# Four instead of three seven-product pairs per slab in the gate and up projections, and another order of the pairs

## The chip, the core and the metric

The kernel runs on one core of one Trainium2 chip. The engines that matter are TensorE (PE, matrix products), VectorE (DVE) and ScalarE (ACT) for element-wise work, GpSimd (POOL) for more of it, and SyncE (SP), which issues the weight transfers. The metric is the device time of one execution in microseconds (us), lower is better: 2799.63 us before, the median of 3 runs (2798.4 to 2800.11).

## The reference, cut to what matters

One layer of a decoder on 256 tokens of width 2048, in float32: a SwiGLU feed-forward part (FF = 5632), a mixer of attention and a state-space scan, and a second SwiGLU part. The change touches the two feed-forward parts alone:

```python
def swiglu(x, w_gate, w_up, w_down):
    return (jax.nn.silu(x @ w_gate) * (x @ w_up)) @ w_down
...
f = swiglu(rms_norm(h, ffn1_pre_g[i]), ffn1_w_gate[i], ffn1_w_up[i], ffn1_w_down[i])
h = h + 0.5 * rms_norm(f, ffn1_post_g[i])
```

## The kernel before, in words

**Float32 in three products.** Each weight tile is split into a high part (ACT, L133, a copy to fp32r) and a low part (DVE, L134, the tile minus its high part); the activations are split in the same way once and kept in "slots". A float32 product is then three matrix products of 128 columns by 512: high by high, high by low, low by high (L389 to L391 in `gate_up`, L140 to L142 in `project`).

**Slabs and units.** FF is cut into 11 slabs of 512 columns. A slab of gate and up sums over 8 units; a unit p is one pair of 128-row blocks of the weights of gate and up, one transfer of 1 MB (128 x 4 x 512). There are two kinds:
- an ordinary unit (N below): 2 blocks x 2 token halves x (gate, up) = 8 float32 products, 24 instructions on PE; two splits of 128x1024 (parts a and b).
- a seven-product unit (S below, those p in the tuple `SP`): the four blocks form a 2x2 matrix product, which is done with 7 products of sums (Strassen's scheme in Winograd's form): 21 instructions on PE. POOL makes the sums of weights, four additions of 128x512 per unit (L371 in `Ahead.make`); three splits of 128x1024 (parts a, c, b) and one of 128x512 (part d), of which b and d read the sums `wsum` and c the block that POOL's fourth addition wrote. The sums of activations are made once, while slab 0 runs (`pair_slots.sums`, L343 to L347), for slab 0 has ordinary units only.

**Banks.** A slab with S units fills all 8 PSUM banks: four for the results g0, u0, g1, u1, and four (p1, p5, p6, p7) for products of the S units. After the last S unit, ACT copies p1 (L428) and DVE makes four combinations from p5, p6, p7 (L430 to L433, "the combinations"); that frees the four. At the slab's end DVE adds these to the results (L440, L442, "the closing adds"), ACT applies Silu (L445), DVE multiplies (L446).

**What sets the order.** `ORDER` is the order of the units in slabs 1 to 10, `SP` which are S. In `ffn` the slabs go in groups (0 to 2, 3 to 5, 6 to 8, 9 and 10); after each group come four slabs of the down projection (`project`). `flush`, called after a unit whose number stands in `after=`, transposes the previous slab's result (L217, tile tp, two banks) into a slot (ACT L197, DVE L198). `Ahead` loads and sums the weights of S units two units ahead, across slabs: two buffers raw7 (tag h) and two buffers wsum (tag xc). A raw7 is free for the next load when its part c is split. Splits of 128x1024 rotate through 4 buffers. Every engine takes its instructions in the order in which they are queued.

```python
            kind = p in SP[:-1]
            if kind not in self.free:
                self.free[kind] = new_slot()
...
            if p in sp:
                raw, e = coming.take()
...
            if len(self.made) == 2 or not self.units:
                return
```

Of the kernel before, what the change touches and what calls it, by code (L numbers as in the profile page):

```python
# [33 lines left out]
EPS = 1e-6  # L34
NFF = FF // S
NP = D // (2 * P)
SP = (2, 4, 6)
ORDER = (0, 2, 1, 4, 3, 6, 5, 7)
AHEAD = 300
LAMBDA_INIT = 0.8 - 0.6 * math.exp(-0.3 * 0)  # L40

# [10 lines left out]
def decoder_layer(ctx: ExitStack, tc: tile.TileContext, x, x_t, cols, rows, post_g, wgu1, wd1, w_in,  # L52
# [91 lines left out]
    def project(xs, w, n, by_token=0):  # L144

        ps = [psm.tile([P, S], F32, name="acc", tag="m") for _ in range(NT)]
        tail = []
        for c in range(len(xs)):  # L150
            raw = raws.tile([P, 4, S], F32, name="raw", tag=turn("raw", 3))
            loaded[0] = nc.sync.dma_start(raw, w(n, c))
            sl = xs[c] = xs[c]() if callable(xs[c]) else xs[c]
            for b in range(2):
                hi, lo = split(raw[:, 2 * b:2 * b + 2], [P, 2, S])
                for jj in range(2):
                    j = 2 * b + jj
                    tail.append((sl, j, hi[:, jj], lo[:, jj], c + j == 0, c == len(xs) - 1 and j == 3))
            if c < len(xs) - by_token:
                for sl_, j, wh, wl, first, last in tail:  # L160
                    for t in range(NT):
                        matmul3(ps[t], sl_, j, t, wh, wl, first, last)
                tail = []
        for t in range(NT):
            for sl_, j, wh, wl, first, last in tail:
                matmul3(ps[t], sl_, j, t, wh, wl, first, last)
        return ps
# [23 lines left out]
    def new_slot():  # L191
        return slots.tile([P, 4, 2, TT], F32R, name="slot")

    def fill(sl, j, src):

        js = slice(j, j + src.shape[1])
        nc.scalar.activation(sl[:, js, 0], src, AF.Copy)  # L197
        nc.vector.tensor_tensor(out=sl[:, js, 1], in0=src, in1=sl[:, js, 0].bitcast(F32), op=ALU.subtract)  # L198
# [10 lines left out]
    def to_slot(src, gain=None):  # L209

        sl = new_slot()
        for b in range(2):
            ps = psm.tile([P, 2, TT], F32, name="tp", tag="m")
            for k in range(2):
                for t in range(NT):
                    j = 2 * b + k
                    nc.tensor.transpose(ps[:, k, t * P:(t + 1) * P], src[t][:, j * P:(j + 1) * P], ident)  # L217
            if gain is None:
                fill(sl, 2 * b, ps)
            else:  # L220
                fill_gain(sl, 2 * b, ps, gain)
        return sl
# [81 lines left out]
    class pair_slots:  # L304
# [8 lines left out]
        def make(self, p, src, gain):  # L313

            g = col[:, gain + 2 * p:gain + 2 * p + 2]
            kind = p in SP[:-1]
            if kind not in self.free:
                self.free[kind] = new_slot()
                sl, k = self.free[kind], 0
            else:  # L320
                sl, k = self.free.pop(kind), 2
            self.at0[p] = sl, k
            if p in SP:
                xg = self.xg[p] = tmp.tile([P, 2, TT], F32, name="xg", tag="t2")
                for i in range(2):
                    nc.scalar.activation(xg[:, i], src[:, i], AF.Copy, scale=g[:, i:i + 1])
                fill(sl, k, xg)
            else:
                self.at[p] = sl, k
                for i in range(2):  # L330
                    nc.scalar.activation(sl[:, k + i, 0], src[:, i], AF.Copy, scale=g[:, i:i + 1])
                    nc.vector.scalar_tensor_tensor(
                        out=sl[:, k + i, 1], in0=src[:, i], scalar=g[:, i:i + 1],
                        in1=sl[:, k + i, 0].bitcast(F32), op0=ALU.mult, op1=ALU.subtract)
# [116 lines left out]
    def ffn(xo, scale, wgu, wd, gi, h_of, fetch=None):  # L451


        nonlocal h
        rs = []
        post = None
        todo = []
        groups = ((0, 3), (3, 6), (6, 9), (9, NFF))
        order = lambda j: ORDER
        coming = Ahead(wgu, [(j, p) for j in range(1, NFF) for p in order(j) if p in SP])  # L460

        def flush():
            if todo:
                hs.append(to_slot(todo.pop()))

        for a, b in groups:
            hs = []
            for j in range(a, b):
                if j == 0:
                    steps = dict(scale)  # L470

                    def behind(i):
                        if i in steps:
                            rs.append(steps[i]())
                        if i - 1 in SP:
                            xo.sums(i - 1)
                        if i >= NP - 2:
                            coming.behind = loaded[0]
                            coming.make()
                            coming.behind = None  # L480
                    todo.append(gate_up(xo.at0, wgu, 0, range(NP), (), None, lambda: rs[-1], fetch,
                                        {i: lambda i=i: behind(i) for i in range(NP)}))
                else:
                    todo.append(gate_up(xo.at, wgu, j, order(j), SP, coming, lambda: rs[-1], after={6: flush}))
            last = b == NFF
            if last:
                h = [hpool.tile([P, D], F32, name=f"h{t}", tag=f"h{t}") for t in range(NT)]
                for t in range(NT):
                    nc.gpsimd.dma_start(h[t], h_of(t))
            if not post:  # L490
                post = PostNorm(gi, 0.5)
                f = post.f

            def final():
                flush()
                return hs[-1]

            lazy = hs + [final]
            for n in range(4):
                pd = project(lazy, lambda n, c: wd[n, a + c], n, by_token=2 if last and n == 3 else 0)  # L500
                part = f[:, :, n * S:(n + 1) * S]
                if not last:
                    for t in range(NT):
                        if a == 0:
                            nc.scalar.activation(part[:, t], pd[t], AF.Copy)
                        else:
                            nc.vector.tensor_tensor(out=part[:, t], in0=pd[t], in1=part[:, t], op=ALU.add)
                else:
                    def get(t):
                        v = tmp.tile([P, S], F32, name="fsum", tag="t2")  # L510
                        nc.vector.tensor_tensor(out=v, in0=pd[t], in1=part[:, t], op=ALU.add)  # L511
                        return v
                    post.slab(n, get)
        return post.finish()
# [30 lines left out]

    steps1 = {i: lambda c=c: square1(c) for c, i in enumerate((1, 2, 4, 5))}
    update = ffn(x1, {**steps1, 7: scale1}, wgu1, wd1, 0, lambda t: x[t * P:(t + 1) * P], fetch1)


# [383 lines left out]
    for t in range(NT):  # L933
        nc.gpsimd.dma_start(hsave2[t], h[t])
    update = ffn(x2, {1: pre_scale}, wgu2, wd2, 2, lambda t: hsave2[t])
    for t in range(NT):
        for c in range(4):
# [57 lines left out]
```

## Time and profile before

| what | value |
|---|---|
| median of 3 runs | 2799.63 us |
| the profiled execution's own time | 2802.36 us |
| its span, first to last instruction | 2800.7 us |
| PE busy | 2769.4 us (99%) |
| DVE busy | 2058.7 us (74%) |
| ACT busy | 1450.1 us (52%) |
| POOL busy | 627.6 us (22%) |
| granted PE clock, mean | 0.996 |

How to read it: busy time is the union of an engine's instructions. Matrix products are pipelined, so one lasts longer (0.39 us) than the distance to the next. The shares are means over stages with different limits; the slabs of gate and up are one stage, the down projection and the mixer are others.

### The profile page before, as it was taken

The numbers are of one execution on the slowest core, as the hardware profiler recorded it, in microseconds if no ns is written. First come the engines' busy times: TensorE is split into PE (matmuls) and PEld (weight loads), VectorE is DVE, ScalarE is ACT, GpSimd is POOL, SyncE is SP. The second block draws the span as 40 slices with busy tenths as digits, with TensorE's granted clock in tenths as the row PEclk, the third lists the DMA queues.
The fourth block names the chain that finished last, engine by engine and source line by source line (L and its number), as shares of the span: only waits on it lengthen the run. The fifth ranks groups of instructions, "written<-read, shape, count | busy, mean of one in ns | idle before, by whom it ended". The sixth has DMA issues, their size and how long they took to land. (4 is left out here: it accounts for less than half of the span.)

```text
span 2800.7 us, 33759 instructions
## 1 busy us (share of the span) xinstructions
PE 2769.4 (99%) x13120; PEld 2312.7 (83%) x13120; DVE 2058.7 (74%) x2311; ACT 1450.1 (52%) x1822; POOL 627.6 (22%) x377
## 2 busy tenths in 40 slices
PE   8999999999999999999999999999999999999998
PEld 6888888888788888888788888888878888888887
DVE  7959969878688877777765565544568869789696
ACT  6545545545565556555444444444465555455454
POOL 2605415322012111111100000000015325236040
PEclk9999999999999999999999999999999999999999
DMA  6555555556555555555554445555556555555554
GB/s 259 206 189 204 198 182 208 195 185 214 198 190 179 189 182 192 184 186 194 188 183 167 176 170 180 203 190 191 193 199 226 194 187 205 196 195 196 195 205 156
DMA packets 77985, 541.50 MB, mean 193 GB/s; under 512 B 8768, under 2 KB 8912, under 8 KB 14080
## 3 DMA queue, kind: packets, MB, share of 16 engines
q1 hardware_dynamic: 73152, 519.08, 52.0%
q0 software_dynamic: 4528, 20.09, 2.0%
q8 instruction: 103, 1.69, 0.2%
q14 instruction: 58, 0.48, 0.0%
q10 hardware_dynamic: 144, 0.17, 0.0%
HBM read 532.94 MB, written 6.36 MB: 193 GB/s over the span
## 5 line engine op out<-in xcount | busy, mean ns | idle before, releaser
L134 DVE TENSOR_TENSOR w_lo<-raw,w_hi 128x1024 fp32r<-128x1024 f32 x978 | 1359.2, 1404 | 628.4 <-ACT w_hi L133 619.2
L133 ACT ACTIVATE w_hi<-raw 128x1024 fp32r<-128x1024 f32 x978 | 1035.7, 1060 | 1050.1 <-PE acc L142 581.6
L140 PE MATMUL acc<-w_hi,slot 128*128 128x512 f32 x1856 | 729.8, 393 | 0.8 <-DVE slot L205 0.2
L141 PE MATMUL acc<-w_lo,slot 128*128 128x512 f32 x1856 | 722.9, 389 | 0.0
L142 PE MATMUL acc<-w_hi,slot 128*128 128x512 f32 x1856 | 720.1, 390 | 0.0
L140 PEld LDWEIGHTS acc<-w_hi,slot 128*128 128x128 f32 x1856 | 348.9, 188 | 78.6 <-ACT slot L197 4.6
L142 PEld LDWEIGHTS acc<-w_hi,slot 128*128 128x128 f32 x1856 | 348.7, 188 | 73.1
L141 PEld LDWEIGHTS acc<-w_lo,slot 128*128 128x128 f32 x1856 | 348.9, 188 | 72.4 <-DVE y L731 1.2
L181 PE MATMUL acc<-slot,w_hi 128*128 128x512 f32 x1280 | 407.8, 399 | 0.2 <-ACT zs L775 0.2
L371 POOL TENSOR_TENSOR wsum<-raw 128x512 f32<-128x512 f32 x120 | 226.7, 1889 | 773.8 <-DMA raw<-in_wgu 766.7
L389 PE MATMUL gu<-w_hi,slot 128*128 128x512 f32 x928 | 363.4, 392 | 7.6 <-ACT w_hi L133 7.6
L390 PE MATMUL gu<-w_lo,slot 128*128 128x512 f32 x928 | 363.2, 391 | 2.6 <-DVE w_lo L134 2.5
L391 PE MATMUL gu<-w_hi,slot 128*128 128x512 f32 x928 | 362.8, 391 | 0.0
L183 PEld LDWEIGHTS acc<-slot,w_lo 128*128 128x128 f32 x1280 | 240.4, 188 | 56.1
L183 PE MATMUL acc<-slot,w_lo 128*128 128x256 f32 x1280 | 252.9, 278 | 0.0
L389 PEld LDWEIGHTS gu<-w_hi,slot 128*128 128x128 f32 x928 | 175.2, 189 | 43.5 <-ACT w_hi L133 7.6
L390 PEld LDWEIGHTS gu<-w_lo,slot 128*128 128x128 f32 x928 | 175.1, 189 | 40.2 <-DVE w_lo L134 4.1
L391 PEld LDWEIGHTS gu<-w_hi,slot 128*128 128x128 f32 x928 | 175.1, 189 | 36.6
L181 PEld LDWEIGHTS acc<-slot,w_hi 128*128 128x128 f32 x1280 | 196.6, 189 | 4.3 <-issue 2.4
L134 DVE TENSOR_TENSOR w_lo<-wsum,w_hi 128x1024 fp32r<-128x1024 f32 x120 | 167.5, 1435 | 19.5 <-ACT w_hi L133 18.9
L389 PE MATMUL gu<-w_hi,sums 128*128 128x512 f32 x420 | 163.4, 389 | 0.0
L390 PE MATMUL gu<-w_lo,sums 128*128 128x512 f32 x420 | 163.4, 389 | 0.0
(228 smaller groups left out, 2153.0 us busy)
## 6 DMA issues: line engine op xcount, KB each, us to landing
raw<-in_wgu SPq DMA_DIRECT2D x175, 1024.0 KB, 4.7
raw<-in_wd SPq DMA_DIRECT2D x88, 1024.0 KB, 4.8
raw<-in_w_in SPq DMA_DIRECT2D x80, 1024.0 KB, 4.8
raw<-in_w_in_t SPq DMA_DIRECT2D x80, 1024.0 KB, 4.8
raw<-in_w_ssm SPq DMA_DIRECT2D x32, 1024.0 KB, 4.7
raw<-in_w_att SPq DMA_DIRECT2D x16, 1024.0 KB, 4.7
raw<-in_w_out SPq DMA_DIRECT2D x16, 1024.0 KB, 4.7
dec<-acsD POOLq DMA_DIRECT2D x16, 512.0 KB, 5.1
```

The source lines that it names most:

```text
L133: split_last["hi"] = nc.scalar.activation(hi[:, js], raw[:, js], AF.Copy)
L134: split_last["lo"] = nc.vector.tensor_tensor(out=lo[:, js], in0=raw[:, js], in1=hi[:, js].bitcast(F32), op=ALU.subtract)
L140: nc.tensor.matmul(ps, xh, wh, start=first, stop=False)
L141: nc.tensor.matmul(ps, xh, wl, start=False, stop=False)
L142: nc.tensor.matmul(ps, xl, wh, start=False, stop=last)
L181: nc.tensor.matmul(ps[f], hi[:, j, wf[f]], sl[:, j], start=b + j == 0, stop=False)
L183: nc.tensor.matmul(ps[f][:, TT:], lo[:, j, wf[f]], sl[:, j, :TT], start=False, stop=b == len(xs) - 1 and j == 3)
L371: sum_last[0] = nc.gpsimd.tensor_tensor(out=o, in0=a, in1=b, op=ALU.add)
L389: nc.tensor.matmul(bank[k], xh, wh, start=done[k] == 1, stop=False)
L390: nc.tensor.matmul(bank[k], xh, wl, start=False, stop=False)
L391: nc.tensor.matmul(bank[k], xl, wh, start=False, stop=done[k] == count[k])
```

## The change: four S units, at places 1, 3, 4 and 6

`SP` becomes (1, 3, 4, 6) and `ORDER` the natural one, so a slab runs N0 S1 N2 S3 S4 N5 S6 N7, where it ran N0 S2 N1 S4 N3 S6 N5 N7. The last S unit is the seventh of eight now and was the sixth. `flush` is called after the last unit and not after the seventh. In `pair_slots.make` all S units share slots, before all but the last.

```diff
-SP = (2, 4, 6)
-ORDER = (0, 2, 1, 4, 3, 6, 5, 7)
+SP = (1, 3, 4, 6)
+ORDER = (0, 1, 2, 3, 4, 5, 6, 7)
...
-            kind = p in SP[:-1]
+            kind = p in SP
...
-                    todo.append(gate_up(xo.at, wgu, j, order(j), SP, coming, lambda: rs[-1], after={6: flush}))
+                    todo.append(gate_up(xo.at, wgu, j, order(j), SP, coming, lambda: rs[-1], after={7: flush}))
```

**First place: DVE in the middle of slab 1.** Names that end in raw7 or wsum on the right are parts of S units (a, c, b, d), those with raw parts of N units. Before:

```order
L134 TENSOR_TENSOR w_lo_628<-raw7_494,w_hi_627 128x1024
L134 TENSOR_TENSOR w_lo_632<-raw7_494,w_hi_631 128x1024
L134 TENSOR_TENSOR w_lo_636<-wsum_495,w_hi_635 128x1024
L134 TENSOR_TENSOR w_lo_640<-wsum_495,w_hi_639 128x512
L134 TENSOR_TENSOR w_lo_674<-raw_671,w_hi_673 128x1024
L134 TENSOR_TENSOR w_lo_678<-raw_671,w_hi_677 128x1024
L134 TENSOR_TENSOR w_lo_706<-raw7_561,w_hi_705 128x1024
L134 TENSOR_TENSOR w_lo_710<-raw7_561,w_hi_709 128x1024
L134 TENSOR_TENSOR w_lo_714<-wsum_562,w_hi_713 128x1024
L134 TENSOR_TENSOR w_lo_718<-wsum_562,w_hi_717 128x512
```

In the changed kernel, in the same stretch:

```order
L134 TENSOR_TENSOR w_lo_641<-raw7_507,w_hi_640 128x1024
L134 TENSOR_TENSOR w_lo_645<-raw7_507,w_hi_644 128x1024
L134 TENSOR_TENSOR w_lo_649<-wsum_508,w_hi_648 128x1024
L134 TENSOR_TENSOR w_lo_653<-wsum_508,w_hi_652 128x512
L134 TENSOR_TENSOR w_lo_685<-raw7_574,w_hi_684 128x1024
L134 TENSOR_TENSOR w_lo_689<-raw7_574,w_hi_688 128x1024
L134 TENSOR_TENSOR w_lo_693<-wsum_575,w_hi_692 128x1024
L134 TENSOR_TENSOR w_lo_697<-wsum_575,w_hi_696 128x512
L134 TENSOR_TENSOR w_lo_731<-raw_728,w_hi_730 128x1024
L134 TENSOR_TENSOR w_lo_735<-raw_728,w_hi_734 128x1024
```

Between two S units stood two splits of an N unit; now two S units follow each other, eight splits in a row, and the N unit comes behind them.

**Second place: DVE from the end of slab 1 into slab 2.** The combinations (L430 to L433), the slot of the previous result (L198) and the closing adds (L440, L442). Before (the splits with raw_808 are of the slab's last unit N7, those with raw_850 of the next slab's first unit):

```order
L134 TENSOR_TENSOR w_lo_811<-raw_808,w_hi_810 128x1024
L430 TENSOR_TENSOR u2_754<-gu_585,c_g0_749 128x512
L134 TENSOR_TENSOR w_lo_815<-raw_808,w_hi_814 128x1024
L431 TENSOR_TENSOR c_g1_750<-gu_589,u2_754 128x512
L432 TENSOR_TENSOR c_u0_751<-gu_581,u2_754 128x512
L433 TENSOR_TENSOR c_u1_752<-gu_581,c_g1_750 128x512
L134 TENSOR_TENSOR w_lo_853<-raw_850,w_hi_852 128x1024
L134 TENSOR_TENSOR w_lo_857<-raw_850,w_hi_856 128x1024
L198 TENSOR_TENSOR slot_793<-tp_794,slot_793 128x2x256
L198 TENSOR_TENSOR slot_793<-tp_801,slot_793 128x2x256
L440 TENSOR_TENSOR c_g0_749<-gu_517,c_g0_749 128x512
L134 TENSOR_TENSOR w_lo_889<-raw7_643,w_hi_888 128x1024
```

And in the changed kernel (raw_873 is the next slab's first unit, raw7_700 its first S unit):

```order
L134 TENSOR_TENSOR w_lo_876<-raw_873,w_hi_875 128x1024
L430 TENSOR_TENSOR u2_811<-gu_598,c_g0_806 128x512
L134 TENSOR_TENSOR w_lo_880<-raw_873,w_hi_879 128x1024
L431 TENSOR_TENSOR c_g1_807<-gu_602,u2_811 128x512
L432 TENSOR_TENSOR c_u0_808<-gu_594,u2_811 128x512
L433 TENSOR_TENSOR c_u1_809<-gu_594,c_g1_807 128x512
L134 TENSOR_TENSOR w_lo_912<-raw7_700,w_hi_911 128x1024
L440 TENSOR_TENSOR c_g0_806<-gu_530,c_g0_806 128x512
L442 TENSOR_TENSOR c_u0_808<-gu_534,c_u0_808 128x512
L440 TENSOR_TENSOR c_g1_807<-gu_538,c_g1_807 128x512
L134 TENSOR_TENSOR w_lo_916<-raw7_700,w_hi_915 128x1024
L198 TENSOR_TENSOR slot_850<-tp_851,slot_850 128x2x256
```

The combinations stood between the splits of the slab's last unit and stand now between those of the next slab's first; three of the closing adds come before the slot is filled, which they followed.

**Third place: PE at the transposes.** The last transpose and the products that follow; a new bank waits for DVE where "waits DVE" stands at a product's first row. Before (the slab's last unit N7 follows):

```order
L217 MATMUL tp_801<-ident_84,sg_504 128x128
L389 MATMUL gu_517<-w_hi_810,slot_390 128x512 [waits Activation_49]
L390 MATMUL gu_517<-w_lo_811,slot_390 128x512
L391 MATMUL gu_517<-w_hi_810,slot_390 128x512
L389 MATMUL gu_521<-w_hi_810,slot_390 128x512
L390 MATMUL gu_521<-w_lo_811,slot_390 128x512
L391 MATMUL gu_521<-w_hi_810,slot_390 128x512
L389 MATMUL gu_525<-w_hi_810,slot_390 128x512
L390 MATMUL gu_525<-w_lo_811,slot_390 128x512
L391 MATMUL gu_525<-w_hi_810,slot_390 128x512
L389 MATMUL gu_529<-w_hi_810,slot_390 128x512
```

In the changed kernel (the next slab's first unit follows):

```order
L217 MATMUL tp_858<-ident_84,sg_517 128x128
L389 MATMUL gu_883<-w_hi_875,slot_111 128x512 [waits DVE_49,Activation_49]
L390 MATMUL gu_883<-w_lo_876,slot_111 128x512
L391 MATMUL gu_883<-w_hi_875,slot_111 128x512
L389 MATMUL gu_887<-w_hi_875,slot_111 128x512 [waits DVE_49]
L390 MATMUL gu_887<-w_lo_876,slot_111 128x512
L391 MATMUL gu_887<-w_hi_875,slot_111 128x512
L389 MATMUL gu_891<-w_hi_875,slot_111 128x512 [waits DVE_49]
L390 MATMUL gu_891<-w_lo_876,slot_111 128x512
L391 MATMUL gu_891<-w_hi_875,slot_111 128x512
L389 MATMUL gu_895<-w_hi_875,slot_111 128x512 [waits DVE_49]
```

The transposes stood ahead of the last unit, which goes on with open banks; they stand now at the slab's end, where four new banks must be free, and all four wait for DVE.

## Rows read from the trace of the kernel before

**Rows 1.** Page, parts 1, 5 and 6: engines; POOL's first sums, 2 per unit; loads

```profile
PE 2769.4 (99%) x13120; PEld 2312.7 (83%) x13120; DVE 2058.7 (74%) x2311; ACT 1450.1 (52%) x1822; POOL 627.6 (22%) x377
...
L371 POOL TENSOR_TENSOR wsum<-raw 128x512 f32<-128x512 f32 x120 | 226.7, 1889 | 773.8 <-DMA raw<-in_wgu 766.7
...
raw<-in_wgu SPq DMA_DIRECT2D x175, 1024.0 KB, 4.7
```

**Rows 2.** Windows of a slab's length, slabs 3 and 4; columns in the first line

```profile
core 0: us, PE busy (x) PEld busy (x) DVE busy (x) ACT busy (x) POOL busy (x), PEclk, DMA share, GB/s
211.00:253.40 42.40, 42.40 (x189) 35.11 (x188) 37.52 (x29) 24.22 (x26) 24.37 (x12) 1.00 0.54 191
257.80:300.20 42.40, 42.40 (x193) 35.20 (x192) 41.95 (x35) 24.50 (x28) 23.87 (x12) 1.00 0.55 199
```

**Rows 3.** Timeline of PE, slab 5: first products of units, transposes, down projection

```profile
314.90 0.39 PE L389 MATMUL gu<-w_hi,slot 128*128 128x512 f32 x1
...
320.34 0.39 PE L389 MATMUL gu<-w_hi,sums 128*128 128x512 f32 x1
...
325.10 0.39 PE L389 MATMUL gu<-w_hi,slot 128*128 128x512 f32 x1
...
330.54 1.04 PE L217 MATMUL tp<-ident,c_g 128*128 128x128 f32 x8
331.33 0.48 PE L389 MATMUL gu<-w_hi,slot 128*128 128x512 f32 x1
...
336.88 0.39 PE L140 MATMUL acc<-w_hi,slot 128*128 128x512 f32 x1
```

**Rows 4.** Timeline of DVE, slab 5: splits, free and beside POOL, and combinations

```profile
301.31 1.22 DVE L134 TENSOR_TENSOR w_lo<-raw,w_hi 128x1024 fp32r<-128x1024 f32 x1
...
304.81 2.32 DVE L134 TENSOR_TENSOR w_lo<-raw,w_hi 128x1024 fp32r<-128x1024 f32 x1
307.05 2.31 DVE L134 TENSOR_TENSOR w_lo<-raw,w_hi 128x1024 fp32r<-128x1024 f32 x1
...
330.63 0.68 DVE L431 TENSOR_TENSOR c_g<-gu,u 128x512 f32<-128x512 f32 x1
331.24 0.67 DVE L432 TENSOR_TENSOR c_u<-gu,u 128x512 f32<-128x512 f32 x1
...
339.96 0.74 DVE L446 SCALAR_TENSOR_TENSOR c_g<-c_u,pre_rstd,c_g 128x512 f32<-128x512 f32 x1
340.62 0.68 DVE L442 TENSOR_TENSOR c_u<-gu,c_u 128x512 f32<-128x512 f32 x1
```

**Rows 5.** Timeline of POOL: the four sums of one unit

```profile
302.51 1.29 POOL L371 TENSOR_TENSOR wsum<-raw 128x512 f32<-128x512 f32 x1 [13.15 <-DMA raw<-in_wgu]
303.88 2.16 POOL L371 TENSOR_TENSOR wsum<-wsum,raw 128x512 f32<-128x512 f32 x1
306.01 2.27 POOL L371 TENSOR_TENSOR wsum<-raw 128x512 f32<-128x512 f32 x1
308.36 2.15 POOL L371 TENSOR_TENSOR raw<-wsum,raw 128x512 f32<-128x512 f32 x1
```

**Rows 6.** Timeline of DVE: part c of the first S unit, slabs 3, 4, 5

```profile
211.99 1.23 DVE L134 TENSOR_TENSOR w_lo<-raw,w_hi 128x1024 fp32r<-128x1024 f32 x1 [1.54 <-ACT w_hi L133]
...
253.75 1.21 DVE L134 TENSOR_TENSOR w_lo<-raw,w_hi 128x1024 fp32r<-128x1024 f32 x1
...
296.32 1.21 DVE L134 TENSOR_TENSOR w_lo<-raw,w_hi 128x1024 fp32r<-128x1024 f32 x1
```

**Rows 7.** Groups by form on DVE, down projection, 344 to 390 us; busy, mean, idle

```profile
L134 DVE TENSOR_TENSOR w_lo<-raw,w_hi 128x1024 fp32r<-128x1024 f32 x17 | 20.8, 1226 | 20.7 <-ACT w_hi L133 20.6
```

**Rows 8.** Timeline of PE, slab 0 of the first part: a gap, the clock after it

```profile
49.15 0.50 PE L390 MATMUL gu<-w_lo,slot 128*128 128x512 f32 x1 [2.53 <-DVE w_lo L134]
...
51.02 0.63 PE L391 MATMUL gu<-w_hi,slot 128*128 128x512 f32 x1
```

**Rows 9.** Windows around that gap, columns as in rows 2

```profile
50.70:54.10 3.40, 3.40 (x10) 2.62 (x9) 2.45 (x4) 1.06 (x1) 0.00 (x0) 0.50 0.87 320
```

**Rows 10.** Timeline of DVE: the sums of activations of one pair, slab 0

```profile
30.96 0.49 DVE L343 TENSOR_TENSOR xf<-xg 128x128 f32<-128x128 f32 x2
...
32.90 0.63 DVE L347 TENSOR_TENSOR sums<-xg,sums 128x256 fp32r<-128x256 f32 x2
...
35.17 0.69 DVE L347 TENSOR_TENSOR sums<-xf,sums 128x512 fp32r<-128x512 f32 x1
```

## The prediction

> **What bounds the kernel now.** I read the page first: PE is busy for 99% of the span, DVE for 74%, POOL for 22% [rows 1]. By that alone the change is a plain gain, since it takes products from PE. So I read next, by windows, the stage in which it acts, a slab of gate and up [rows 2]: there PE is busy for all of 42.4 us, but DVE for 41.95 us of the same 42.4. The reader is to see that the slabs have two engines at their limit, and the page's 74% is a mean with the down projection, where DVE waits for half its time (20.7 of 46 us idle) [rows 7]. Only the first slab of a group, where nothing of an earlier slab is left to close, has slack (37.52 us). Then the timelines of PE, DVE and POOL inside a slab [rows 3 to 5].
>
> **What PE gains.** An N unit begins at 314.90 and the S unit after it at 320.34, the next N at 325.10 [rows 3]: 24 products take 5.44 us, 21 take 4.76, 0.227 us each. One more S unit saves 0.68 us a slab; 20 slabs have S units (slabs 1 to 10 of two parts): 13.6 us. PE's need falls from 42.4 to 41.7 us a slab.
>
> **What DVE pays.** Its distances, start to start [rows 4]: a split of 128x1024 stands at 1.22 us and fills 1.14 (the next starts before it ends); a split of half that size 0.6; an instruction on a PSUM bank (L430 to L433, L440, L442, L198) 0.6 (330.63 to 331.24); L446 0.7. A slab before: 19 splits (5 N x 2, 3 S x 3) x 1.14 = 21.7; 3 halves = 1.8; 10 instructions on banks and two L446 = 7.4. Sum 30.9. It was busy for 41.95, so 11.05 us are something else. The same rows show what: beside POOL's sums a split lasts 2.31 us instead of 1.22, 1.1 more, and its neighbours are as long; POOL's sums stretch likewise, from 1.29 to some 2.2 [rows 4, 5]. At 1.1 us a hit, 11.05 us are 10 hits by 12 POOL sums a slab. DVE's instructions on banks keep their 0.68 us beside POOL's fourth sum, and so two sums of the third unit hit nothing.
>
> The changed slab has 20 splits (4 x 2 + 4 x 3) = 22.8, 4 halves = 2.4, the same 7.4: 32.6 us. And 16 POOL sums. How many hit? I follow the queue from the end of part c of S1, which frees the buffer for S4's weights. The load lands after 4.7 us [rows 1], and POOL then works for 8.0 us (302.51 to 310.51) [rows 5]. S4's four sums fall on N2 and S3 (4 hits, splits alone in the queue). Part c of S3 ends at about 14 us; S6's sums run from 19 to 27, on S4 and N5 (4 hits). The sums for the next slab's S1 run from 27 to 35, on S6 and N7 (4). Those for its S3 run from 35 to 43, where two full splits and the last of N7 stand among the combinations (3). So 15 hits, 16.5 us, and a DVE slab of 49.1 us. Bounds: the share before, 10 of 12, gives 13.3 hits and 47.3 us; all 16 give 50.2, and with a wait of 0.5 us for S6's sums (they end at 27, just when DVE wants part c of S6) 50.7. I take 49.1, since with two S units in a row more splits and fewer instructions on banks stand beside POOL. This is far above PE's 41.7 us: DVE becomes the bound, and PE's gain of 13.6 us is worth nothing there.
>
> [...]
>
> **The sum.** I count on DVE from part c of a slab's first S unit to that of the next. Before, the ends are 213.22, 254.96 and 297.53 [rows 6]: 41.7 us from the first slab of a group to the second, 42.6 to the third. And from the last one to the first product of the down projection (336.88) [rows 3]: 39.35.
> - Second to third slab: 49.1 - 42.6 = +6.5. First to second: the first slab has no closing adds, L446 or slot behind its part c, 3.2 us less, but DVE waits for PE's buffers there; I take 1.3 of the 3.2 (bounds 0 and 3.2): 47.8 - 41.7 = +6.1.
> - End of a group: the first product of the down projection needs a bank that L431 frees, its second one that L433 frees. In DVE's order two bank instructions, a split, three closing adds and a split (1.2 + 1.14 + 1.8 + 1.14 = 5.3) lie between L431 and the place of the next part c. So it starts at 49.1 - 5.3 + 0.5 for the second bank = 44.3 us: +5.0. Before, the four banks came free a unit ahead.
> - Last group (slabs 9 and 10): in slab 10 POOL has no next slab to serve, 7 hits less, and PE sets the time again; but the transposes now come after N7, and the slot that the down projection starts with is filled behind them by DVE (two splits, three closing adds, two slot fills, partly before): I take 42.3 us, +3.0 (bounds +1.5 and +4).
>
> Groups of one part: slabs 1, 2: 6.1 + 5.0 = 11.1; slabs 3 to 5 and 6 to 8: 6.1 + 6.5 + 5.0 = 17.6 each; slabs 9, 10: 6.1 + 3.0 = 9.1. Sum 55.4; two parts: 110.8 us.
> - [...] PE now has about 7 us a slab to stand still; inside a group its slack hides the loss, at the 8 ends nothing does: 0 to 14 us, taken 4.
> - One more pair's sums of activations in slab 0: five small instructions, three splits, 1.9 us free [rows 10]. In the first part DVE starves PE there already (the gap of rows 8): +2 (0 to 5). In the second part the first slab of a group and slab 0 have room: 0.
> - Loads (as many bytes as before): nothing, as PE, busy for all of the window [rows 2], waits for none. POOL at 16 sums is at 33 of 49 us: no bound.
>
> Together +116.8 us on the profiled execution's 2802.4 = 2919. It stands 2.8 us above the median; so 2916 for the median.
>
> **Rivals.**
> 1. DVE keeps up, and the kernel is faster. PE's 41.7 us leave 41.7 - 32.6 = 9.1 us for hits, 8 of 16. If POOL's sums fell where DVE works on banks or waits, half of them would hit nothing, and 13.6 us are gained: 2786. Against it: 10 of 12 hit today, and DVE is the fuller the less PE waits. It decides at 8 hits. Chance 0.04; between 8 and 9 hits the two effects cancel, no change, 2800: 0.02.
> 2. The change acts, DVE bounds, but the hits are fewer (10 to 12, slabs of 43.6 to 45.8 us) and the ends of groups cheap (some 10 us in all): 1.4 to 3.6 us over today's 42.2 in 12 intervals is 17 to 43, with the ends 27 to 53: some 2840, 2827 to 2853. For it: rows 2 show PE never waiting today, so DVE's 41.95 us may hold some time that it gives back under pressure. Chance 0.12.
> 3. The clock. PE stands still in several short waits around the end of a slab. If that takes the clock to the lower level for 40% of each slab, PE needs 41.7 / 0.8 = 52.1 us, 3 more than DVE, in 20 slabs: some 2975. For it: rows 8 and 9. Against it: there it followed a single gap of 2.53 us, and the waits that I work out at a slab's end are 1 to 2 us each with products between. Chance 0.12.
>
> **How the numbers follow.** Forecast 0.70: 2916, its own range 2860 to 2960: with 47.3 us a slab, all 3.2 us of the first slab given back, and the low ends elsewhere the sum is some 60 us, 2860; with 50.7 us, no shift, and the high ends of clock and slab 0 it is 170, 2970. Of its 0.70 some 0.06 lie above 2960. To hold 0.8 the range reaches into rival 2: 2845 to 2960. Slower by over 0.2% (5.6 us, about what a measurement of this kernel tells from none): forecast and rivals 2 and 3, 0.94; the same 0.02; faster 0.04.
>
> **What would show it.** Right: PE's share falls to about 95%, DVE is busy to 98% or more in windows of slabs 4, 5, 7, 8; a slab there lasts 48 to 50 us; PE's idle time is released by w_lo of DVE in the middle of slabs, and by L431 to L440 at their ends; 80 units of sums. Wrong: PE without idle time in these windows (rival 1); splits of 2.3 us fewer than 12 a slab (rival 2); a granted clock clearly below 1.00 over whole slabs (rival 3); POOL's sums ending late and ACT waiting for them for microseconds (then the step that says the sums are in time is wrong).

## The result, and the profile after

The changed kernel took 2891.44 us (median of 4 runs, 2890.46 to 2894.09), the kernel before 2799.32 us (median of 4, 2798.4 to 2800.11): a ratio of 1.0332, interval 1.0318 to 1.0346. It is slower by 92 us; 2916 had been predicted, with a range of 2845 to 2960. The profiled execution took 2894.09 us; its span grew from 2800.7 to 2892.4 us.

The page of the changed kernel, parts 1 and 5, answers to [rows 1]:

```profile
PE 2797.6 (97%) x13060; PEld 2290.4 (79%) x13060; DVE 2172.3 (75%) x2363; ACT 1475.5 (51%) x1870; POOL 810.7 (28%) x457
...
L371 POOL TENSOR_TENSOR wsum<-raw 128x512 f32<-128x512 f32 x160 | 327.8, 2049 | 697.2 <-DMA raw<-in_wgu 623.0
```

PE has 60 products fewer (13060 for 13120) and POOL 80 additions more (457 for 377; the line shows two of the four per unit, so 80 units): the change did what it says. DVE shows 75% of the span where it showed 74%. In the page nothing has become a bound; the windows of slabs 3 and 4, cut at the same event (the end of part c of S1), say otherwise. Columns as in [rows 2]:

```profile
core 0: us, PE busy (x) PEld busy (x) DVE busy (x) ACT busy (x) POOL busy (x), PEclk, DMA share, GB/s
219.98:267.69 47.71, 45.93 (x197) 36.09 (x196) 45.24 (x33) 25.40 (x28) 32.18 (x16) 1.00 0.50 176
267.69:314.53 46.84, 42.03 (x179) 31.91 (x178) 43.98 (x35) 25.20 (x30) 33.65 (x16) 1.00 0.51 180
```

Before, from the first slab of a group to the second took 41.7 us and to the third 42.6 [rows 6]; now 47.71 and 46.84. PE stands still for 1.8 and 4.8 us of them, and the granted clock stays at 1.00. The waits of PE over the whole span (engine and line, what ended the wait, sum in us, times, longest) say for whom:

```profile
PE gu L390 <- DVE w_lo L134: 43.2, 66, 2.5
PE gu L389 <- ACT w_hi L133: 8.2, 6, 7.3
PE gu L389 <- DVE c_g L440: 7.7, 6, 1.4
PE acc L140 <- DVE c_g L431: 6.0, 6, 1.0
PE gu L389 <- DVE c_g L431: 2.6, 6, 0.4
```

Before, PE waited once for a low part, 2.5 us; now 66 waits for low parts make 43.2 us. (The row on w_hi holds a wait of 7.3 us at the kernel's start; it was 7.6 before.) That is DVE as the bound in the middle of slabs, and the rows on L431 and L440 are the ends of slabs and groups. These rows show less than PE lost: its idle time grew from 31.3 to 94.8 us, by 63.5, while the span grew by 91.7 with 60 products fewer to do. A product is drawn for 0.39 us and its successor stands 0.227 behind it, so a pause shows as idle only where it is longer than the overlap, and the rest counts as busy. DVE's groups by form in slab 4 (267.69 to 314.53) show what it is busy with:

```profile
L134 DVE TENSOR_TENSOR w_lo<-raw,w_hi 128x1024 fp32r<-128x1024 f32 x16 | 26.5, 1696 | 2.3 <-ACT w_hi L133 2.3
L134 DVE TENSOR_TENSOR w_lo<-wsum,w_hi 128x1024 fp32r<-128x1024 f32 x4 | 7.5, 1872 | 0.6 <-ACT w_hi L133 0.6
L134 DVE TENSOR_TENSOR w_lo<-wsum,w_hi 128x512 fp32r<-128x512 f32 x4 | 4.9, 1228 | 0.0
```

A split that takes 1.22 us alone [rows 4] has a mean of 1.70 here: POOL's sums hit it. And DVE itself waited 2.3 us, which the prediction had not seen. The timeline of POOL in that slab (start, us, instruction, idle before) shows the origin, the first line in particular, which answers to the first of [rows 5]:

```profile
272.48 4.57 POOL L371 TENSOR_TENSOR wsum<-raw 128x512 f32<-128x512 f32 x1 [9.51 <-DMA raw<-in_wgu]
277.12 2.16 POOL L371 TENSOR_TENSOR wsum<-wsum,raw 128x512 f32<-128x512 f32 x1
279.24 1.74 POOL L371 TENSOR_TENSOR wsum<-raw 128x512 f32<-128x512 f32 x1
281.06 2.15 POOL L371 TENSOR_TENSOR raw<-wsum,raw 128x512 f32<-128x512 f32 x1
```

And DVE beside it (x4: four splits back to back, merged):

```profile
271.27 4.62 DVE L134 TENSOR_TENSOR w_lo<-raw,w_hi 128x1024 fp32r<-128x1024 f32 x4
276.48 3.35 DVE L134 TENSOR_TENSOR w_lo<-wsum,w_hi 128x1024 fp32r<-128x1024 f32 x2 [0.59 <-ACT w_hi L133]
...
284.34 1.23 DVE L134 TENSOR_TENSOR w_lo<-raw,w_hi 128x1024 fp32r<-128x1024 f32 x1 [2.27 <-ACT w_hi L133]
```

Four splits in 4.62 us are four at their full speed: in that stretch POOL's first addition got next to nowhere, and it ended only after DVE had paused for 0.59 us. (Spans on POOL are rough; the splits at full speed and the delay that follows bear this one out.) So the four sums ended at 283.21, and the split of the block that the fourth writes (part c of S4, at 284.34) came 2.27 us late. The row names ACT, but ACT had stood waiting too. The waits of ACT over the whole span have it 30 times, where the kernel before has no such row:

```profile
ACT w_hi L133 <- POOL raw L371: 90.1, 30, 5.3
```

At a group's end, PE's last transposes and the first products of the down projection, answering to the last of [rows 3]:

```profile
355.81 1.03 PE L217 MATMUL tp<-ident,c_g 128*128 128x128 f32 x8
357.83 0.47 PE L140 MATMUL acc<-w_hi,slot 128*128 128x512 f32 x1 [0.99 <-DVE c_g L431]
...
358.94 0.50 PE L140 MATMUL acc<-w_hi,slot 128*128 128x512 f32 x1 [0.17 <-DVE c_u L433]
```

### The profile page after: what moved, and what is told of

Same layout as the page of the kernel before. It is cut to its first block, busy times and chain, and to the rows that moved or that the text cites. A ratio compares the mean times of both kernels' runs of the same rounds, so it can differ in the third digit from the quotient of the medians.

```text
span 2892.4 us, 33861 instructions
## 1 busy us (share of the span) xinstructions
PE 2797.6 (97%) x13060; PEld 2290.4 (79%) x13060; DVE 2172.3 (75%) x2363; ACT 1475.5 (51%) x1870; POOL 810.7 (28%) x457
## 5 line engine op out<-in xcount | busy, mean ns | idle before, releaser
L134 DVE TENSOR_TENSOR w_lo<-raw,w_hi 128x1024 fp32r<-128x1024 f32 x978 | 1397.9, 1445 | 616.4 <-ACT w_hi L133 609.0
L371 POOL TENSOR_TENSOR wsum<-raw 128x512 f32<-128x512 f32 x160 | 327.8, 2049 | 697.2 <-DMA raw<-in_wgu 623.0
L390 PE MATMUL gu<-w_lo,slot 128*128 128x512 f32 x768 | 305.6, 398 | 27.7 <-DVE w_lo L134 27.3
L389 PE MATMUL gu<-w_hi,slot 128*128 128x512 f32 x768 | 303.0, 396 | 19.2 <-DVE c_g L440 7.7
L391 PE MATMUL gu<-w_hi,slot 128*128 128x512 f32 x768 | 300.7, 392 | 0.0
L134 DVE TENSOR_TENSOR w_lo<-wsum,w_hi 128x1024 fp32r<-128x1024 f32 (+1 forms) x160 | 239.8, 1538 | 14.8 <-ACT w_hi L133 14.8
L390 PE MATMUL gu<-w_lo,sums 128*128 128x512 f32 x560 | 225.0, 402 | 17.1 <-DVE w_lo L134 15.9
L389 PE MATMUL gu<-w_hi,sums 128*128 128x512 f32 x560 | 218.8, 391 | 1.0 <-ACT w_hi L133 0.9
L391 PE MATMUL gu<-w_hi,sums 128*128 128x512 f32 x560 | 218.4, 390 | 0.0
L390 PEld LDWEIGHTS gu<-w_lo,slot 128*128 128x128 f32 x768 | 144.7, 188 | 74.9 <-DVE w_lo L134 47.2
L389 PEld LDWEIGHTS gu<-w_hi,slot 128*128 128x128 f32 x768 | 144.7, 189 | 59.3 <-DVE c_g L440 10.3
```

The source lines that it names most:

```text
L134: split_last["lo"] = nc.vector.tensor_tensor(out=lo[:, js], in0=raw[:, js], in1=hi[:, js].bitcast(F32), op=ALU.subtract)
L371: sum_last[0] = nc.gpsimd.tensor_tensor(out=o, in0=a, in1=b, op=ALU.add)
L389: nc.tensor.matmul(bank[k], xh, wh, start=done[k] == 1, stop=False)
L390: nc.tensor.matmul(bank[k], xh, wl, start=False, stop=False)
L391: nc.tensor.matmul(bank[k], xl, wh, start=False, stop=done[k] == count[k])
```

## Experiments

The theory: POOL's reads slow DVE's splits, DVE is the bound of a slab, and both the number of sums and their place matter. The rivals: the new order by itself (late combinations, transposes behind the last unit), or the four units' work on PE, ACT and DVE without any collision.

**1. The sums of weights gone.** After, with POOL writing zeros in place of adding:

```diff
-    sum_last[0] = nc.gpsimd.tensor_tensor(out=o, in0=a, in1=b, op=ALU.add)
+    sum_last[0] = nc.gpsimd.memset(o, 0.0)
```

> The changed kernel with POOL's four additions per S unit replaced by writes of zeros to the same tiles (the sums of weights are left out). Theory (collisions of DVE's splits with POOL's additions make the loss): without reads on POOL there are no hits, DVE needs 32.6 us a slab, PE its 41.7, and splits stay at 1.22 us in the slabs; what is left is PE's gain of 13.6 us less the waits for banks at the slabs' ends, 0 to 10 us: 2785 to 2800 us, 92 to 106 below the changed kernel. Rival (the moved flush and the later banks at the slab's end, or two S units in a row, make the loss): this order is the same here, so at least half of the 92 us stays: 2845 us or more.

Measured: 2786.09 us (2785.26 to 2788.07), ratio to before 0.9957, interval 0.994 to 0.9974. All of the loss is gone and 12.5 us are gained. That this is near the 13.6 that PE saves is in part chance: part c of slab 1's first S unit ends at 56.84 us here, at 61.40 before. The two traces differ by 15.8 us (the one before is of an execution 2.7 us above the median), and 4.6 of them stand in slab 0, where POOL's sums hit DVE too (before, the split at 37.62 us takes 2.31) and 1.7 us were lost by the clock (3.4 us at 0.50 [rows 9]); 11.2 are left for all that follows. A window of a slab's length, and DVE's splits in it:

```profile
257.00:298.00 41.00, 41.00 (x187) 34.02 (x186) 33.18 (x36) 25.70 (x29) 7.85 (x16) 1.00 0.57 201
```

```profile
L134 DVE TENSOR_TENSOR w_lo<-raw,w_hi 128x1024 fp32r<-128x1024 f32 x16 | 19.4, 1223 | 3.2 <-ACT w_hi L133 3.0
L134 DVE TENSOR_TENSOR w_lo<-wsum,w_hi 128x1024 fp32r<-128x1024 f32 x4 | 4.9, 1226 | 4.7 <-ACT w_hi L133 4.6
L134 DVE TENSOR_TENSOR w_lo<-wsum,w_hi 128x512 fp32r<-128x512 f32 x4 | 2.7, 684 | 0.0
```

POOL still has 16 instructions in the window, but they read nothing, and a split is back at 1223 ns. DVE's need, 33.2 us, is near what the prediction worked out without hits (32.6). Against these rows the splits of slab 4 in the changed kernel are longer by 16 x 0.473, 4 x 0.646 and 4 x 0.544 us: 12.3 us of hits. Where nothing collides, the late combinations and transposes can take little: 2.4 us lie between the 11.2 and PE's 13.6. The zeros also end POOL's delays, for the 16 writes of the window take 7.85 us, some half a microsecond each: ACT's row on POOL is gone. So the run shows what the sums on POOL cost in all, and not the hits apart from the delays.

**2. The new order with three units.** After, with places 1, 3 and 6:

```diff
-SP = (1, 3, 4, 6)
+SP = (1, 3, 6)
...
-            kind = p in SP
+            kind = p in SP[:-1]
```

> Three S units again, at places 1, 3 and 6 of the natural order, flush after the last unit as in the changed kernel: the new slab end without the fourth unit. Theory: DVE needs 30.9 us and some 10 to 11 hits, 42 to 43 us a slab, beside PE's 42.4, so the slabs hardly grow; the ends of slabs cost up to 4 us in six groups: 2800 to 2830. Rival (slab end makes the loss): 2860 or more.

Measured: 2804.3 us (2802.58 to 2806.21), ratio 1.0021, interval 1.0011 to 1.003. The order with three units, the last S unit and the transposes later by a unit, costs 6 us; the rest comes with the fourth unit. Two S units in a row come with it as well; no run has four units without them, but experiment 1 shows that by themselves, without POOL's reads, they cost nothing like it.

**3. Four units, each place earlier.** After, with the places 1, 2, 4, 5 and the transposes ahead of the last unit again:

```diff
-SP = (1, 3, 4, 6)
+SP = (1, 2, 4, 5)
...
-lambda: rs[-1], after={7: flush}))
+lambda: rs[-1], after={6: flush}))
```

> Four S units at places 1, 2, 4 and 5, flush after the seventh unit as before: the fourth unit without the new slab end. Theory: DVE is as full as in the changed kernel, intervals of 46 to 49 us, only the ends of groups become cheaper (by up to 4 us in six of them): 2865 to 2895. Rival (slab end makes the loss): 2787 to 2815.

Measured: 2896.21 us (2893.36 to 2897.93), ratio 1.0349, interval 1.0333 to 1.0364: just above the expected 2865 to 2895, so the cheaper ends that were counted on did not show in the time. With the transposes back ahead of the last unit it is no better. A window and PE's largest wait:

```profile
257.00:298.00 41.00, 37.91 (x159) 29.00 (x158) 40.90 (x32) 22.46 (x26) 27.86 (x14) 1.00 0.54 191
```

```profile
PE gu L390 <- DVE w_lo L134: 69.8, 87, 2.8
```

DVE is busy for 40.90 of 41.00 us: the loss stands in the middle of slabs now, so DVE's total decides and not the place at which PE waits for it.

**4. The same additions on DVE.** If the price is the collision, the sums can go to the engine that they hit: 16 additions at an estimated 0.6 us, the distance that the prediction read for a half split, are 9.6 us a slab, against the 12.3 that the hits took in slab 4, and POOL's delays go. Just ahead of the unit's splits, POOL's four additions deleted:

```diff
+                    with tc.issue_after(split_last["lo"].ins):
+                        split_last["lo"] = nc.vector.tensor_tensor(out=o, in0=a, in1=b, op=ALU.add)
```

> The changed kernel with the four additions on DVE itself, just ahead of each S unit's splits, none on POOL. Theory: 16 additions of 128x512 at 0.6 us are 9.6 us, less than the 14 us that hits and waits for POOL cost now: DVE needs 32.6 + 9.6 = 42.2 us a slab, PE 41.7; about 2795 to 2815, splits back at 1.22 us. Rival (DVE is the bound by the number of its instructions, and hits are only stretched durations in its shadow): 9.6 us more on DVE per slab makes it slower than the changed kernel, 2950 or more.

Measured: 2799.9 us (2798.45 to 2801.49), ratio 1.0005, interval 0.9996 to 1.0014: the loss is gone, the gain isn't there. Window, a wait of PE, and one of ACT:

```profile
257.00:298.00 41.00, 40.24 (x179) 32.32 (x179) 40.72 (x51) 23.66 (x29) 0.00 (x0) 1.00 0.58 206
```

```profile
PE gu L391 <- ACT w_hi L133: 13.2, 13, 8.0
```

```profile
ACT w_hi L133 <- DVE raw L377: 199.3, 68, 3.7
```

Of PE's 13.2 us, 8.0 are the wait at the kernel's start. From the end of part c of S1 in slab 4 (250.07) to the same in slab 5 (291.45) there are 41.38 us now: DVE is busy for 40.95 of them, 3.0 less than 43.98, and idle for 0.43 in place of 2.86. So DVE's shorter work and the end of the delays have about equal shares in what is won back there. ACT can split part c only when the fourth addition is done, and that stands directly ahead; but DVE is at its limit as well, and this run doesn't tell which of the two keeps back the gain.

**5. Both.** The additions on DVE as in 4, and the places of 3 with its transposes ahead of the last unit:

```diff
-SP = (1, 3, 4, 6)
+SP = (1, 2, 4, 5)
...
-lambda: rs[-1], after={7: flush}))
+lambda: rs[-1], after={6: flush}))
...
+                        split_last["lo"] = nc.vector.tensor_tensor(out=o, in0=a, in1=b, op=ALU.add)
```

> Four S units at places 1, 2, 4 and 5, flush after the seventh unit, additions on DVE just ahead of each S unit's splits. Theory: DVE 42.2 us, PE 41.7, no waits for banks at the ends of slabs: 2788 to 2800, a little below the same with places 1, 3, 4, 6 (2799.9). Rival (two S units in a row, now 4.8 us of additions and 8 splits, starve PE in the middle of the slab): 2805 or more.

Measured: 2806.95 us (2804.16 to 2807.64), ratio 1.0029, interval 1.0018 to 1.0041: the theory's 2788 to 2800 failed, and the rival's 2805 or more held. PE's wait for w_hi is 20.0 us in 21 times, more than in the kernel with places 1, 3, 4, 6. Places 1, 2 and 4, 5 are two pairs of S units in a row, where 1, 3, 4, 6 has one; behind an S unit no N unit hides the next one's additions. That is read from the order, not tested by itself.

**6 to 8. The additions one unit sooner.** A unit's four additions are queued ahead of the splits of the unit before it, so that ACT finds them done:

```diff
+            if sp and order[(i + 1) % NP] in sp:
+                coming.sum()
             if p in sp:
...
             self.make()
+            self.sum()
+            self.summed = False
             return self.made.pop(0)
```

With places 1, 3, 4, 6:

> The changed kernel's places (1, 3, 4, 6), additions on DVE, but ahead of the splits of the unit before each S unit. Theory: the same DVE time as with the additions just ahead, but ACT no longer waits for the addition that part c needs; the 5.7 us in which PE waited for w_hi go: 2790 to 2798. Rival (DVE's total of 42.2 us against PE's 41.7 is what PE waits for): 2798 to 2804, no change.

Measured: 2809.3 us (2808.53 to 2810.43), ratio 1.0039, interval 1.0025 to 1.0053. Both expectations missed. The wait for w_hi went as it should, but others came: the waits of PE and ACT name low parts and the combinations and closing adds of DVE (in these kernels the lines of after have moved down by up to 10; L450 is the closing add):

```profile
PE gu L398 <- DVE w_lo L134: 11.6, 24, 0.7
```

```profile
ACT w_hi L133 <- DVE raw L384: 32.0, 24, 1.5
ACT c_g L455 <- DVE c_g L450: 31.8, 12, 2.9
```

The same with places 1, 2, 4, 5 and the transposes ahead of the last unit:

```diff
-SP = (1, 3, 4, 6)
+SP = (1, 2, 4, 5)
...
-lambda: rs[-1], after={7: flush}))
+lambda: rs[-1], after={6: flush}))
```

> Places 1, 2, 4 and 5, flush after the seventh unit, additions on DVE ahead of the splits of the unit before. Theory: both gains together, 2786 to 2796, the fastest. Rival (the additions now wait for the load, which is issued only when the S unit two before has split its part c, and hold up DVE): 2805 or more.

Measured: 2788.79 us (2787.56 to 2790.8), ratio 0.9966, interval 0.9954 to 0.9979: faster than both kernels, by 9.6 us than before. Window, and PE's waits for the two halves of a split:

```profile
257.00:298.00 41.00, 41.00 (x184) 33.50 (x183) 40.51 (x51) 23.77 (x28) 0.00 (x0) 1.00 0.57 204
```

```profile
PE gu L397 <- ACT w_hi L133: 7.8, 1, 7.8
...
PE gu L398 <- DVE w_lo L134: 1.8, 5, 0.5
```

PE is busy for all of the window, DVE for 40.51 us of 41.00: there is half a microsecond a slab to spare, and the fourth unit pays. The two kernels differ in the places and in where the transposes stand; that the late combinations of place 6 are what cost the other one its 20 us is what its waits suggest, and no run takes that apart.

The same edit made in the kernel before, with its three units and its order:

> The kernel before with three S units, additions on DVE ahead of the unit before. Theory: DVE needs 30.9 + 7.2 = 38.1 us a slab where PE needs 42.4, so DVE gets slack and the time stays, 2795 to 2803: where PE is the bound, taking the collisions away gives nothing. Rival (PE is slowed by DVE's 98% in some hidden way): 2785 or less.

Measured: 2796.64 us (2795.34 to 2798.09), ratio 0.9994, interval 0.9985 to 1.0003. Moving the additions is worth little by itself while PE is the bound: 1.7 us of the 9.6, with an interval that reaches from a loss of 0.8 to 4.2. In the traces of all five runs with the additions on DVE slab 0 is 4.1 to 4.4 us shorter than before, so this small gain stands there and not in the slabs that the change is about. The fourth unit with its places is worth the other 7.9 us (2796.64 to 2788.79), of PE's 13.6.

## Why the prediction held, by its steps

- **PE's gain is 13.6 us and worth nothing.** Held: with the sums on POOL none of it came, and without their reads 12.5 us did, some of that in slab 0 (experiment 1).
- **DVE's slab is 32.6 us and hits.** Held in kind: without hits DVE is busy for 33.2 us in 41; with them it bounds (experiments 1 and 3).
- **15 hits of 1.1 us, 49.1 us from the second slab to the third.** Mis-sized: 46.84. DVE's 43.98 busy us are 12.3 of hits, about 11, and 31.7 of its own work: the 32.6 counted two fills of the slot (L198), and in the changed order these lie behind part c, from 314.45, at the cut of the window. On top come 2.9 us of idle time. So the hits were put 4.2 us too high (16.5), DVE's own work 0.9 too high, and the idle time 2.9 too low (none, with 0.5 as its bound): together the 2.2 us by which 49.1 was too long. That it came so near is in part luck, as errors of opposite sign cancel.
- **The sums are in time.** Failed, for S4's unit: its sums had been placed on N2 and S3, "4 hits". The first of them did not share the time with the splits, as [rows 4] and [rows 5] show it, but stood still behind them, and part c of S4 was 2.27 us late. That would also explain the missing hits, as a split beside a starved addition is not slowed: the four splits of N2 and S3, on which four hits had been counted, ran at full speed (4.62 us for all four).
- **First slab to second, 47.8.** Measured 47.7 in six of the eight groups; in those of slabs 1 and 2 it is 46.81 and 47.09. The wait for PE's buffers is there too: DVE is idle for 2.47 us of 47.71, behind ACT, which waits for PE's products (L391).
- **End of a group, +5.0.** 43.30 us from part c of S1 to the first product of the down projection (314.53 to 357.83), where 39.35 were before, and the second bank 0.43 later still (358.94 is 1.11 behind 357.83, where three products take 0.68): +4.4. The waits are those that were named, for L431 and L433. Last groups came out at +8.6 and +8.4, where 9.1 was the sum.
- **Clock, 4 us.** Nothing: no run shows the term. The granted clock is 1.00 in every window from slab 1 on (56.00 to 760.00 us in the first part, 2150.00 to 2870.00 in the second), though PE stands still for up to 4.8 us in one, in pieces of 1.4 at most.
- **Slab 0, +2.** -1.2. PE's gap came back, 2.52 us at 52.26 after 2.53 before, but the 3.4 us at a granted clock of 0.50 [rows 8, 9], a loss of 1.7, did not: the clock stayed at 1.00 behind the gap. So slab 0 grew by some 0.5 us and won 1.7 that the change has no part in. Both, the gap and the clock behind it (columns as above):

```profile
52.26 0.50 PE L390 MATMUL gu<-w_lo,slot 128*128 128x512 f32 x1 [2.52 <-DVE w_lo L134]
```

```profile
52.26:56.00 3.74, 3.74 (x16) 3.11 (x17) 3.74 (x4) 1.51 (x2) 0.00 (x0) 1.00 0.27 55
```


The sum as it came out, by groups in order of time: -1.2 (slab 0), 8.0, 14.7, 14.8 and 8.6 in the first part, 8.9, 14.8, 14.7 and 8.4 in the second: 91.7 us, the growth of the span. The forecast's 116.8 was 25 too high: 10 us from the four intervals between second and third slabs, 5 from the groups of slabs 1 and 2, 7 from clock and slab 0, and 3 from the other groups' ends and first intervals.

Of the signs that were named, PE's waits for w_lo in the middle of slabs and for L431 to L440 at their ends came, and so did the 80 units. PE's share is 97% and not 95, because of the pauses that count as busy. "DVE busy to 98%" missed, because the idle time for POOL counts against it (43.98 of 46.84 is 94%), and "48 to 50 us" missed by little. Two signs that were named for being wrong came as well: ACT waits for POOL for microseconds, and eight splits of slab 4 last over 2.2 us where fewer than twelve were to speak for rival 2. The second was a poor sign, for the kernel before has seven such splits in its slab 4, and shorter stretches make up the rest. Rival 3, the clock, is out. Rival 2 had the number of hits right (10 to 12) and the cheap ends wrong.

Beside POOL's writes a split took 1223 ns (experiment 1), beside its additions 1696 in the mean of slab 4. The first addition there stood still for longer than the rest of one split, 1.22 us at most: it lasts from 272.48 to 277.05, and the four splits end at 275.89. That it stood still until then is an estimate from the 1.16 us that are left, near the 1.29 us of an addition alone [rows 5].

## What to carry to other kernels

Work given to a side engine is to be priced by what it does to the engine that it collides with: here sixteen additions on POOL took 12.3 us of DVE in a slab and kept it idle for 2.9, and made on DVE itself they take about 10 (0.69 us each in the window of experiment 4, at a distance of some 0.6, as instructions of that length have it in [rows 4]) and delay no one through POOL. When an engine's mean over the span looks free, cut a window of one stage at one recurring event: 74% on the page of the kernel before was 99% in the second slab of a group (41.95 of 42.40 us [rows 2]). Where such additions stand in the queue is to be tried with the order, not apart from it: one unit sooner took places 1, 2, 4, 5 from 2806.95 to 2788.79 us and places 1, 3, 4, 6 from 2799.9 to 2809.3.

## What was not expected of the hardware

The collision of DVE and POOL is not even. In the kernel before each side is stretched, a split from 1.22 to 2.31 us and an addition from 1.29 to 2.2 [rows 4, 5], and so are four splits in a row in the changed kernel (9.02 us from 319.43). But in some places where splits follow each other without a pause, POOL's addition stands still: it lasts 4.57 us in the slab shown and 4.38 to 4.55 in five others, one each in slabs 4, 7 and 10 of both parts, up to 4.5 in experiment 2, and up to 7.56 us in experiment 3, while none in the kernel before lasted over 2.4. What decides between the two, no run here shows.

Two gaps of nearly the same length were followed by different granted clocks. In slab 0 the clock fell to 0.50 behind a gap of 2.53 us in the kernel before [rows 8, 9], and stayed at 1.00 behind one of 2.52 in the changed kernel; what decides, no run here shows.
